# Row variance of an 8192 x 8192 matrix: whole 32 KiB rows per load, a quarter of each row on ScalarE, the last tile in pieces

## The chip, the cores and the metric

The kernel runs on one core of a Trainium2 chip. The metric is the device time of one execution in microseconds (us); the numbers quoted are medians of several runs. The profile is one execution recorded by the hardware; its span is about 1.8 us shorter than the device time, because launch and end lie outside it.

Engines in the profile: DVE is VectorE, ACT is ScalarE, POOL is GpSimd, PE and PEld are TensorE's matmul and weight load, SP is SyncE. A "q" behind the name is the engine's instruction queue, here issuing DMA transfers. All transfers of the core run on 16 DMA engines. A packet is the piece that one DMA engine moves at a time, here one stretch of one row; a chunk is the 512 columns that one `bn_stats` reads.

## The reference

```
def setup_inputs():
    return {"x": np.random.randn(8192, 8192).astype(np.float32)}

def reference(x):
    return np.var(x, axis=1)
```

So 268.4 MB are read once and 32 KB are written.

## The kernel before

128 rows, one per partition, make a tile; there are 64 tiles of 4 MiB. Each tile is loaded in two halves (16 KiB per row), one from SyncE's queue and one from ScalarE's. VectorE does all the arithmetic: 16 `bn_stats` of 512 columns (count, mean and sum of squared deviations of the even and of the odd elements) and one `bn_aggr`, which merges them to mean and variance. GpSimd copies the variance into a column of `var_all`. At the end TensorE transposes `var_all` so that the store writes 64 rows of 512 bytes.

```
    data = ctx.enter_context(tc.tile_pool(name="data", bufs=4))
    ...
    def issue_dma(t):
        xt = data.tile([P, nsub, FMAX], mybir.dt.float32)
        for c in range(CH):                                   # CH = 2
            lo = c * spc
            hi = lo + spc
            dma_eng[c % 2].dma_start(out=xt[:, lo:hi, :], in_=x_t[t, :, lo:hi, :])
    ...
    def compute(t):
        ...
        for j in range(nsub):                                 # nsub = 16
            nc.vector.bn_stats(out=st[:, j, :], in_=xt[:, j, :])
        nc.vector.bn_aggr(out=mv, in_=st)
        nc.gpsimd.tensor_copy(out=var_all[:, t : t + 1], in_=mv[:, 1:2])
    ...
    nc.tensor.transpose(vp, var_all, ident)
    nc.scalar.copy(vs, vp)
    nc.sync.dma_start(out=out_t, in_=vs)
```

## Time and profile before

| | before |
|---|---|
| device time, median (range) | 655.37 us (655.24 to 655.69) |
| span of the profile | 653.6 us |
| VectorE busy | 636.2 us, 97% |
| a tile on VectorE, start to start | 9.93 us |
| a tile on most of the 16 DMA engines | 9.79 us |

Lines of the page of the kernel before: its busy times, bytes moved per second in 40 slices of the span, its DMA queues, and the two costly groups (busy us, mean ns of one, idle time before them and what ended it).

```profile
span 653.6 us, 1512 instructions
PE 0.4 (0%) x1; PEld 0.1 (0%) x1; DVE 636.2 (97%) x1088; ACT 1.5 (0%) x2; POOL 12.4 (2%) x70
...
GB/s 369 433 430 425 427 432 428 425 431 428 427 428 430 427 427 430 427 427 428 428 426 431 427 429 427 426 429 428 428 427 430 427 428 429 429 425 430 429 222 2
...
q14 instruction: 12, 0.10, 0.0%
...
L61 DVE BATCH_NORM_STATS2 st<-xt 128x6 f32<-128x512 f32 x1024 | 610.1, 673 | 13.6 <-DMA xt<-in_x_dram 13.6
L63 DVE BATCH_NORM_AGGREGATE mv<-st 128x2 f32<-128x96 f32 x64 | 36.4, 570 | 0.1
```

VectorE waits for data only 13.6 us in all, nearly all of it for the first tile. So VectorE sets the pace. But the loads run at about 428 GB/s all the time until about 629 us, so there is little to gain below VectorE. (The mean of one `bn_stats`, 673 ns, is longer than its share of the pace, because two of them overlap; from start to start it is 0.59 us.)

The end of the kernel before, from its timeline (start us, duration us, engine, line, operation; in brackets the idle time before it):

```profile
630.32 9.53 DVE L61 BATCH_NORM_STATS2 st<-xt 128x6 f32<-128x512 f32 x16
...
640.26 8.93 DVE L61 BATCH_NORM_STATS2 st<-xt 128x6 f32<-128x512 f32 x15
...
649.29 0.59 DVE L63 BATCH_NORM_AGGREGATE mv<-st 128x2 f32<-128x96 f32 x1
649.94 0.18 POOL L64 COPY var_all<-mv 128x1 f32<-128x1 f32 x1 [9.36 <-DVE mv L63]
...
650.93 0.55 SPq L77 DMA_DIRECT2D out_dram<-vs  x1
```

The last two lines of the same kernel's issue list: kilobytes each, and median us from issue to landing.

```profile
xt<-in_x_dram SPq DMA_DIRECT2D x64, 2048.0 KB, 28.9
out_dram<-vs SPq DMA_DIRECT2D x1, 32.0 KB, 1.8
```

The store of 64 rows of 512 bytes takes 1.8 us from issue to landing. Between issue and the end of the span lie 2.65 us.

One view needs the raw records. A load is split over the 16 DMA engines, and each adds one to the load's semaphore (a counter that the waiting engine watches) when its part has landed. The trace holds the time of each of the 16, so one sees whether one engine lags:

| landing of (us) | first of 16 | 15th | 16th |
|---|---|---|---|
| tile 0, second half | 12.71 | 12.96 | 13.00 |
| tile 63, second half | 629.36 | 630.67 | 638.46 |

Fifteen engines are done at about 630 us and one 8 us later. The records say why: at nine times, about 70 to 80 us apart, an 8 KiB packet of kind "instruction" runs on queue 14, and the 16 KiB data packet next to it takes 1273 ns where others take 611 to 615. The last of the 16 completions steps back by about 0.96 us each time; over the whole run the mean is (9.10 - 0.29) / 9 = 0.98 us per fetch. VectorE has 1150 instructions with its waits, about nine blocks of 128. (The page counts 12 packets on queue 14. Beside the other three a data packet takes 961 to 1024 ns, and the last completion does not step back.)

### The profile page before, as it was taken

The page shows a single profiled execution, that of the slowest core. Times are in us where ns is not written, and L with a number is a line of the kernel's source. Part 1 is how long each engine was busy: PE and PEld are TensorE (multiplying, and loading weights), DVE is VectorE, ACT ScalarE, POOL GpSimd, SP SyncE. Part 2 cuts the span into 40 slices and gives each one's busy share as a digit, 9 for nine tenths or more (in the row PEclk, how much of TensorE's full clock was granted, in tenths as well). Part 3 has the DMA queues.
Part 4 walks back from the last instruction along what each step waited for, and adds up shares of the span by engine and source line. Part 5 has one row for each costly group of instructions (what it writes and reads, how often), then busy time and mean ns, then how long its engine had stood idle before and what let it go on. Part 6 is the DMA issues. An engine that isn't in the chain of part 4 may idle for free.

```text
span 653.6 us, 1512 instructions
## 1 busy us (share of the span) xinstructions
PE 0.4 (0%) x1; PEld 0.1 (0%) x1; DVE 636.2 (97%) x1088; ACT 1.5 (0%) x2; POOL 12.4 (2%) x70
## 2 busy tenths in 40 slices
PE   0000000000000000000000000000000000000000
PEld 0000000000000000000000000000000000000000
DVE  2999999999999999999999999999999999999997
ACT  0000000000000000000000000000000000000000
POOL 0000000000000000000000000000000000000000
DMA  8999999999999999999999999999999999999950
GB/s 369 433 430 425 427 432 428 425 431 428 427 428 430 427 427 430 427 427 428 428 426 431 427 429 427 426 429 428 428 427 430 427 428 429 429 425 430 429 222 2
DMA packets 18524, 268.57 MB, mean 411 GB/s; under 512 B 2064, under 2 KB 2128, under 8 KB 2128
## 3 DMA queue, kind: packets, MB, share of 16 engines
q1 hardware_dynamic: 9296, 134.25, 48.4%
q10 hardware_dynamic: 9216, 134.22, 48.2%
q14 instruction: 12, 0.10, 0.0%
HBM read 268.44 MB, written 0.03 MB: 411 GB/s over the span
## 4 chain that ended last, share of the span: by engine, by line
DVE 88%; DMA 6%; issue 5%; SPq 0%; PE 0%; ACT 0%; POOLq 0%; POOL 0%
DVE st L61 82%; DMA xt<-in_x_dram 6%; DVE mv L63 5%; SPq L54 0%; PE vp L74 0%; ACT vs L76 0%; POOLq L103 0%; POOL var_all L64 0%
## 5 line engine op out<-in xcount | busy, mean ns | idle before, releaser
L61 DVE BATCH_NORM_STATS2 st<-xt 128x6 f32<-128x512 f32 x1024 | 610.1, 673 | 13.6 <-DMA xt<-in_x_dram 13.6
L63 DVE BATCH_NORM_AGGREGATE mv<-st 128x2 f32<-128x96 f32 x64 | 36.4, 570 | 0.1
L64 POOL COPY var_all<-mv 128x1 f32<-128x1 f32 x64 | 11.7, 183 | 637.1 <-DVE mv L63 637.1
L76 ACT ACT_TABLE_LOAD x1 | 1.3, 1283 | 609.9 <-DMA xt<-in_x_dram 609.9
L74 PE MATMUL vp<-ident,var_all 128*64 128x128 f32 x1 | 0.4, 421 | 650.2 <-POOL var_all L64 650.2
L76 ACT COPY vs<-vp 64x128 f32<-64x128 f32 x1 | 0.3, 258 | 39.5 <-PE vp L74 39.5
masks.py:199 POOL TENSOR_SCALAR_AFFINE_SELECT ident<-ident 128x128 f32<-128x128 f32 x1 | 0.3, 292 | 0.1
L74 PEld LDWEIGHTS vp<-ident,var_all 128*64 128x64 f32 x1 | 0.1, 128 | 650.2 <-POOL var_all L64 650.2
masks.py:197 POOL MEMSET ident<- 128x128 f32 x1 | 0.2, 204 | 0.3 <-POOLq L92 0.3
L92 POOL MEMSET const-float32-0.0<- 128x1 f32 x1 | 0.1, 98 | 0.2 <-issue 0.2
L92 POOL MEMSET const-bfloat16-1.0<- 128x1 bf16 x1 | 0.1, 101 | 0.0
L92 POOL MEMSET const-uint8-127<- 128x1 uint8 x1 | 0.1, 101 | 0.0
L92 POOL MEMSET const-float32-1.0<- 128x1 f32 x1 | 0.1, 98 | 0.0
## 6 DMA issues: line engine op xcount, KB each, us to landing
xt<-in_x_dram ACTq DMA_DIRECT2D x64, 2048.0 KB, 29.1
xt<-in_x_dram SPq DMA_DIRECT2D x64, 2048.0 KB, 28.9
out_dram<-vs SPq DMA_DIRECT2D x1, 32.0 KB, 1.8
```

Of the source, the lines that this page charges most:

```text
L61: nc.vector.bn_stats(out=st[:, j, :], in_=xt[:, j, :])
L63: nc.vector.bn_aggr(out=mv, in_=st)
L64: nc.gpsimd.tensor_copy(out=var_all[:, t : t + 1], in_=mv[:, 1:2])
L74: nc.tensor.transpose(vp, var_all, ident)
L76: nc.scalar.copy(vs, vp)
L92: nc = _bacc.Bacc("TRN2", target_bir_lowering=False, num_devices=1)
```

## The change

The intent: take a quarter of the arithmetic off VectorE, make packets larger, and let little work remain behind the last byte.

```diff
-    CH = 2
-            dma_eng[c % 2].dma_start(out=xt[:, lo:hi, :], in_=x_t[t, :, lo:hi, :])
+    data = ... bufs=6
+        nc.sync.dma_start(out=xt, in_=x_t[t])               # 32 KiB rows, SyncE only
...
-        for j in range(nsub):
-            nc.vector.bn_stats(out=st[:, j, :], in_=xt[:, j, :])
+        for c in range(DC):                                 # DC = 12
+            bn(st, c, xt[:, o + c * F : o + (c + 1) * F])
+        k = st[:, 1:2]                                      # a mean from the first chunk
+        src = xt[:, o + DC * F : o + m]                     # the last 2048 columns
+        nc.scalar.activation(out=junk, in_=src, func=ACTF.Identity, bias=k, scale=-1.0,
+                             accum_out=s12[:, 0:1])         # sum of (k - x)
+        nc.scalar.activation(out=junk, in_=src, func=ACTF.Square, bias=k, scale=-1.0,
+                             accum_out=s12[:, 1:2])         # sum of (k - x)^2
+        ...   five GpSimd operations on 128x1: count, mean and squared deviations as one more entry of st
...
+    pieces = [4096, 2048, 1024, 512, 256, 256]              # the last tile
+    for w in pieces:
+        nc.sync.dma_start(out=xt[:, lo : lo + w], in_=x_t[t, :, lo : lo + w])
+    ...   63 tiles' variances: transpose and store as before
+    while lo < m:                                           # all 17 chunks on VectorE
+        w = F if m - lo > 512 else 256
+        bn(stl, i, xt[:, lo : lo + w])
+    nc.vector.bn_aggr(out=mv, in_=stl[:, 0 : i * 6])
+    nc.vector.tensor_copy(out=var_last[:, 0:1], in_=mv[:, 1:2])
+        nc.sync.dma_start(out=out_last[t], in_=var_last)    # 128 pieces of 4 bytes
```

More of the change, by code (lines that the diff above doesn't have):

```diff
@@ L7 @@
 from concourse._compat import with_exitstack
+FP32 = mybir.dt.float32
+ACTF = mybir.ActivationFunctionType
+ALU = mybir.AluOpType
 @with_exitstack
@@ L19 @@
     n, m = x.shape
-    FMAX = nc.vector.BN_STATS_FMAX
-    assert m % FMAX == 0
-    nsub = m // FMAX
-    assert n % P == 0
-    ntiles = n // P
-    x_t = x.rearrange("(t p) (s f) -> t p s f", p=P, f=FMAX)
-    out_t = out.rearrange("(t p) -> t p", p=P)
-    data = ctx.enter_context(tc.tile_pool(name="data", bufs=4))
-    stats = ctx.enter_context(tc.tile_pool(name="stats", bufs=8))
+    F = nc.vector.BN_STATS_FMAX
+    J = 1
+    NT = n // (P * J)
+    C = m // F
+    AC = 4
+    DC = C - AC
@@ L33 @@
+    NA = AC * F
+    T3 = 3
+    x_t = x.rearrange("(t p j) f -> t p (j f)", p=P, j=J)
+    out_tj = out.rearrange("(t q) -> t q", q=P * J)
+    out_last = out.rearrange("(t p j) -> t p j", p=P, j=J)
+    data = ctx.enter_context(tc.tile_pool(name="data", bufs=6))
+    stats = ctx.enter_context(tc.tile_pool(name="stats", bufs=6))
+    small = ctx.enter_context(tc.tile_pool(name="small", bufs=6))
     singles = ctx.enter_context(tc.tile_pool(name="singles", bufs=1))
     psum = ctx.enter_context(tc.tile_pool(name="psum", bufs=1, space=bass.MemoryType.PSUM))
-    outp = ctx.enter_context(tc.tile_pool(name="outp", bufs=1))
@@ L37 @@
-    var_all = singles.tile([P, ntiles], mybir.dt.float32)
-    ident = singles.tile([P, P], mybir.dt.float32)
-    make_identity(nc, ident)
-    dma_eng = [nc.sync, nc.scalar]
-    CH = 2
-    spc = nsub // CH
-    xts = [None] * ntiles
-    LOOK = 3
-    def issue_dma(t):
-        xt = data.tile([P, nsub, FMAX], mybir.dt.float32)
-        for c in range(CH):
-            lo = c * spc
-            hi = lo + spc
-            dma_eng[c % 2].dma_start(out=xt[:, lo:hi, :], in_=x_t[t, :, lo:hi, :])
-        xts[t] = xt
@@ L57, in compute @@
-    def compute(t):
-        xt = xts[t]
-        st = stats.tile([P, nsub, nc.vector.BN_STATS_DIM], mybir.dt.float32)
-        for j in range(nsub):
-            nc.vector.bn_stats(out=st[:, j, :], in_=xt[:, j, :])
-        mv = stats.tile([P, nc.vector.BN_AGGR_DIM], mybir.dt.float32)
-        nc.vector.bn_aggr(out=mv, in_=st)
-        nc.gpsimd.tensor_copy(out=var_all[:, t : t + 1], in_=mv[:, 1:2])
-    for t in range(ntiles):
-        issue_dma(t)
-        if t >= LOOK:
-            compute(t - LOOK)
@@ L70, with bn @@
-    for t in range(ntiles - LOOK, ntiles):
-        compute(t)
-    vp = psum.tile([ntiles, P], mybir.dt.float32)
-    nc.tensor.transpose(vp, var_all, ident)
-    vs = outp.tile([ntiles, P], mybir.dt.float32)
-    nc.scalar.copy(vs, vp)
-    nc.sync.dma_start(out=out_t, in_=vs)
+    var_all = singles.tile([P, J, NT], FP32)
+    var_last = singles.tile([P, J], FP32)
+    junk = psum.tile([P, NA], FP32)
+    def bn(st, at, src):
+        nc.vector.bn_stats(out=st[:, at * 6 : at * 6 + 6], in_=src)
@@ new lines, in row_stats @@
+    def row_stats(xt, j):
+        st = stats.tile([P, DC * 6 + T3], FP32)
+        s12 = small.tile([P, 2], FP32)
+        tmp = small.tile([P, 2], FP32)
+        o = j * m
+        for c in range(DC):
[6 more added lines that the diff above has]
+                             accum_out=s12[:, 1:2])
+        b = DC * 6
+        nc.gpsimd.memset(st[:, b : b + 1], float(NA))
+        nc.gpsimd.tensor_scalar(out=tmp[:, 0:1], in0=s12[:, 0:1], scalar1=1.0 / NA, scalar2=0.0,
+                                op0=ALU.mult, op1=ALU.add)
+        nc.gpsimd.tensor_tensor(out=st[:, b + 1 : b + 2], in0=k, in1=tmp[:, 0:1], op=ALU.subtract)
+        nc.gpsimd.tensor_tensor(out=tmp[:, 1:2], in0=s12[:, 0:1], in1=tmp[:, 0:1], op=ALU.mult)
+        nc.gpsimd.tensor_tensor(out=st[:, b + 2 : b + 3], in0=s12[:, 1:2], in1=tmp[:, 1:2], op=ALU.subtract)
+        return st
@@ new lines, in finish @@
+    def finish(st, t, j):
+        mv = small.tile([P, 2], FP32)
+        nc.vector.bn_aggr(out=mv, in_=st)
+        nc.gpsimd.tensor_copy(out=var_all[:, j, t : t + 1], in_=mv[:, 1:2])
+    pending = []
+    for t in range(NT - 1):
+        xt = data.tile([P, J * m], FP32, name="xt")
+        nc.sync.dma_start(out=xt, in_=x_t[t])
+        for j in range(J):
+            st = row_stats(xt, j)
+            pending.append((st, t, j))
+            if len(pending) > 1:
+                finish(*pending.pop(0))
@@ new lines @@
+    t = NT - 1
+    xt = data.tile([P, m], FP32, name="xt")
+    pieces = [4096, 2048, 1024, 512, 256, 256]
+    lo = 0
+    for w in pieces:
+        nc.sync.dma_start(out=xt[:, lo : lo + w], in_=x_t[t, :, lo : lo + w])
+        lo += w
+    finish(*pending.pop(0))
+    ident = singles.tile([P, P], FP32)
+    make_identity(nc, ident)
+    vs = singles.tile([NT - 1, P, J], FP32)
+    for j in range(J):
+        vp = psum.tile([NT - 1, P], FP32, name="vp")
+        nc.tensor.transpose(vp, var_all[:, j, 0 : NT - 1], ident)
+        nc.scalar.copy(vs[:, :, j], vp)
@@ new lines @@
+    nc.sync.dma_start(out=out_tj[0 : NT - 1], in_=vs)
+    stl = stats.tile([P, (C + 1) * 6], FP32, name="stl")
+    lo, i = 0, 0
+    while lo < m:
+        w = F if m - lo > 512 else 256
+        bn(stl, i, xt[:, lo : lo + w])
+        lo += w
+        i += 1
+    mv = small.tile([P, 2], FP32)
+    nc.vector.bn_aggr(out=mv, in_=stl[:, 0 : i * 6])
+    nc.vector.tensor_copy(out=var_last[:, 0:1], in_=mv[:, 1:2])
+    with nc.allow_non_contiguous_dma(reason="two values per partition"):
+        nc.sync.dma_start(out=out_last[t], in_=var_last)
```

## The prediction

> **What bounds it now.** Two limits are almost level. By the groups view VectorE (DVE) is busy 636.2 of 653.6 us: 16 bn_stats and one bn_aggr per 128-row tile, started every 9.93 us by the timeline; after its first tile it is never starved (13.6 us of DMA wait in all). The loads are hardly faster. In the DMA records each 16 KiB packet takes 611 to 615 ns, so a tile lands every 9.79 us on most of the 16 DMA engines. One engine loses about 0.96 us nine times (landings of a tile's 16 completions), each time just after an 8 KiB "instruction" packet on queue 14, about every 70 us; these fit VectorE's 1147 instructions in blocks of 128. That engine lands the last tile at 638.5, the others at about 630 (the stretch table shows DMA share 0.06, one engine of 16, after 630). VectorE starts that tile at 640.3 and the span ends at 653.6. So taking a quarter of the rows off VectorE does not buy 25%: the loads take over.
>
> **What changes.**
> - VectorE: 12 bn_stats and one bn_aggr, 12 x 0.59 + 0.49 = 7.6 us per tile, under the tile pitch. It will idle about 2 us per tile, waiting for DMA.
> - ScalarE: two passes over 2048 elements. The Trainium skill, "ScalarE: Activation LUTs", section on what ACT_TABLE_LOAD costs, gives about 1.99 us for one with a pointer bias (no run here shows it yet); about 4.3 us a tile with the accumulator reads, by estimate. GpSimd: five small ops near the measured 0.18 us. Both finish before VectorE's 12 chunks do, off the critical path.
> - DMA: 8 packets of 32 KiB per engine and tile rather than 16 of 16 KiB, and one completion write rather than two. The skill, "DMA: Bandwidth & Descriptors", "Where 436 GB/s comes from", gives 435.2 GB/s, that is 602 ns per 16 KiB; measured is 612. Taking the difference, 9 ns, as a cost per packet (the completion writes are also recorded at 9 ns), a 32 KiB packet takes about 1214 ns and a tile 9.72 us (estimate). That gives 62 x 0.07 = 4.5 us. One queue instead of two should cost nothing.
> - Instruction fetches: VectorE will have about 960 instructions, so 7 fetches, 6.7 us of lag on its engine.
> - Tail: the last tile is cut into shrinking pieces, but ScalarE does not help there. VectorE meets tile 62 whole at its landing, spends 7.1 + 0.5 us on it, then has all 17 chunks of the last tile: 15 x 0.59 + 2 x 0.33 = 9.5 us. So it ends about 7 us after the last piece landed, and the small pieces gain nothing.
>
> **Sum.** Tile 0 lands at 12.9; tile 62 at 12.9 + 62 x 9.72 + 6.7 = 622; VectorE done with chunks at 639.2; last aggregate, copy, store and closing 3.6 us (before: 649.2 to 653.6, less transpose and ScalarE copy): span about 643. Launch time outside the span 1.8 us as before: 644.6 us, a ratio of 0.984. Range 639 to 650. Chances: faster by over 2% 0.27, within 2% 0.69, slower 0.04.
>
> **Signs.** VectorE busy falls to about 500 us with some 120 us of DMA wait; 32 KiB packets near 1214 ns; tile pitch 9.72; about 7 instruction fetches followed by long packets on one engine; last piece landed about 632; VectorE running unbroken for about 17 us at the end; ScalarE busy about 270 us.
>
> **What would make it wrong.** A single queue leaving gaps between packets (pitch near 9.9: about 650); fetches that cost more or less behind 32 KiB packets, or extra lag on one engine from GpSimd's and ScalarE's added instructions; VectorE waiting for GpSimd in every aggregate.

## More of the kernel before

The experiments ran in three groups on three chips, with the kernel before beside each group.

The order of instructions on an engine need not be that of the program text: the tool that builds the kernel schedules them.

## The result

The changed kernel takes 649.84 us (649.6 to 650.48); the kernel before takes 655.37. The ratio is 0.9916, 95% interval 0.9902 to 0.993. (Ratios are the mean time of one kernel's fast runs over that of the other's fast runs of the same rounds, so not quite the ratio of the medians.)

Lines of the changed kernel's page that answer to those shown before:

```profile
span 647.9 us, 2020 instructions
PE 0.5 (0%) x1; PEld 0.2 (0%) x1; DVE 496.1 (77%) x838; ACT 265.5 (41%) x254; POOL 59.5 (9%) x384
...
GB/s 388 421 433 440 421 433 439 423 431 437 425 437 433 425 438 431 425 441 429 423 446 427 421 447 422 425 445 425 425 446 425 425 445 423 426 445 423 425 243 2
...
q14 instruction: 16, 0.13, 0.0%
...
L50 DVE BATCH_NORM_STATS2 st<-xt 128x6 f32<-128x512 f32 x756 | 454.8, 679 | 137.5 <-DMA xt<-in_x_dram 137.5
L63 ACT ACTIVATE junk<-xt,st 128x2048 f32<-128x2048 f32 x63 | 124.2, 1972 | 346.9 <-DVE st L50 346.9
```

VectorE lost 140 us of work and gained 124 us of waiting for data: it is no longer the limit in the loop. The loads are, and they are hardly faster than VectorE was.

The end of the changed kernel, from its timeline:

```profile
622.03 7.22 DVE L50 BATCH_NORM_STATS2 st<-xt 128x6 f32<-128x512 f32 x12 [1.90 <-DMA xt<-in_x_dram]
...
629.16 0.68 DVE L50 BATCH_NORM_STATS2 stl<-xt 128x6 f32<-128x512 f32 x1
...
630.15 9.00 DVE L50 BATCH_NORM_STATS2 stl<-xt 128x6 f32<-128x512 f32 x16
...
639.18 0.62 DVE L119 BATCH_NORM_AGGREGATE mv<-stl 128x2 f32<-128x102 f32 x1
639.83 0.15 DVE L120 COPY var_last<-mv 128x1 f32<-128x1 f32 x1
640.01 0.37 SPq L122 DMA_DIRECT2D out_dram<-var_last  x1
```

VectorE works with hardly a pause from 622.03 to 639.98. And its two stores in the issue list (for the first the profile gives no landing):

```profile
out_dram<-vs SPq DMA_DIRECT2D x1, 31.5 KB
out_dram<-var_last SPq DMA_DIRECT2D x1, 0.5 KB, 7.0
```

The last store moves 512 bytes and takes 7.0 us. The completions in the records:

| landing of (us) | first of 16 | 15th | 16th |
|---|---|---|---|
| tile 0 | 12.46 | 12.83 | 12.87 |
| tile 62 | 614.77 | 617.44 | 621.93 |
| last piece of tile 63 | 624.88 | 627.40 | 632.11 |
| last store | 642.94 | 646.58 | 646.97 |

So the 5.5 us gained come from three parts. In the loop, the landing of tile 62 at 621.93 us replaces VectorE's pace; at the end, VectorE has 29 chunks left from there, and 7.0 us of that work lies behind the last byte (632.11); and the store takes back 5 us.

### The profile page after: what moved, and what is told of

Same layout as the page of the kernel before. It is cut to its first block, busy times and chain, and to the rows that moved or that the text cites. A ratio compares the mean times of both kernels' runs of the same rounds, so it can differ in the third digit from the quotient of the medians.

```text
span 647.9 us, 2020 instructions
## 1 busy us (share of the span) xinstructions
PE 0.5 (0%) x1; PEld 0.2 (0%) x1; DVE 496.1 (77%) x838; ACT 265.5 (41%) x254; POOL 59.5 (9%) x384
## 4 chain that ended last, share of the span: by engine, by line
DVE 72%; another core or an unknown queue 17%; DMA 8%; issue 1%; DVEq 0%; SPq 0%
DVE st L50 66%; DMA xt<-in_x_dram 8%; DVE mv L78 4%; DVE stl L50 1%; SPq L84 0%; DVEq L78 0%; DVEq L50 0%; DVE mv L119 0%; DVE var_last L120 0%
## 5 line engine op out<-in xcount | busy, mean ns | idle before, releaser
L50 DVE BATCH_NORM_STATS2 st<-xt 128x6 f32<-128x512 f32 x756 | 454.8, 679 | 137.5 <-DMA xt<-in_x_dram 137.5
L63 ACT ACTIVATE junk<-xt,st 128x2048 f32<-128x2048 f32 x63 | 124.2, 1972 | 346.9 <-DVE st L50 346.9
L65 ACT ACTIVATE junk<-xt,st 128x2048 f32<-128x2048 f32 x63 | 124.2, 1972 | 2.0
L69 POOL TENSOR_SCALAR tmp<-s 128x1 f32<-128x1 f32 x63 | 12.1, 192 | 311.1 <-ACT junk L63 311.1
L78 DVE BATCH_NORM_AGGREGATE mv<-st 128x2 f32<-128x75 f32 x63 | 31.1, 494 | 6.4
L79 POOL COPY var_all<-mv 128x1 f32<-128x1 f32 x63 | 11.7, 185 | 153.8 <-DVE mv L78 153.8
L73 POOL TENSOR_TENSOR st<-s,tmp 128x1 f32<-128x1 f32 x63 | 12.1, 191 | 100.3 <-ACT junk L65 100.3
L71 POOL TENSOR_TENSOR st<-st,tmp 128x1 f32<-128x1 f32 x63 | 12.1, 191 | 5.2
L72 POOL TENSOR_TENSOR tmp<-s,tmp 128x1 f32<-128x1 f32 x63 | 12.0, 191 | 0.0
L63 ACT ACTIVATION_READ_ACCUMULATOR junk<-xt,st 128x1 f32 x63 | 11.8, 187 | 0.0
L65 ACT ACTIVATION_READ_ACCUMULATOR junk<-xt,st 128x1 f32 x63 | 11.7, 186 | 0.0
L50 DVE BATCH_NORM_STATS2 stl<-xt 128x6 f32<-128x512 f32 (+1 forms) x17 | 9.7, 645 | 0.0
L63 ACT ACT_TABLE_LOAD x1 | 1.3, 1283 | 12.9 <-DMA xt<-in_x_dram 12.9
L68 POOL MEMSET st<- 128x1 f32 x63 | 6.2, 99 | 0.3 <-POOLq L137 0.3
```

The source lines that it names most:

```text
L50: nc.vector.bn_stats(out=st[:, at * 6 : at * 6 + 6], in_=src)
L63: nc.scalar.activation(out=junk, in_=src, func=ACTF.Identity, bias=k, scale=-1.0, accum_out=s12[:, 0:1])
L65: nc.scalar.activation(out=junk, in_=src, func=ACTF.Square, bias=k, scale=-1.0, accum_out=s12[:, 1:2])
L68: nc.gpsimd.memset(st[:, b : b + 1], float(NA))
L69: nc.gpsimd.tensor_scalar(out=tmp[:, 0:1], in0=s12[:, 0:1], scalar1=1.0 / NA, scalar2=0.0, op0=ALU.mult, op1=ALU.add)
L71: nc.gpsimd.tensor_tensor(out=st[:, b + 1 : b + 2], in0=k, in1=tmp[:, 0:1], op=ALU.subtract)
```

## The experiments

The theory after the result: (1) VectorE limits the kernel before, and larger packets alone gain nothing; (2) in the changed kernel the loads limit the loop, at a rate set by a fixed cost per packet plus one DMA engine delayed by VectorE's instruction fetches; (3) the special last tile costs more than it saves, through VectorE's serial work and above all through the 4-byte store. Times below are medians; the kernel before ran beside each group, at 655.33 to 655.38.

### e1 and e8: the loads alone

e1 changes one line of the kernel before:

```diff
-    CH = 2
+    CH = 1
```

> The kernel before with only its loads changed: one 32 KiB row per partition on the SyncE queue. Theory (VectorE sets the pace, 9.93 us a tile): loads land faster, about 9.72 us a tile and the last tile near 634 instead of 638.5, but the time stays at 655, within 1 us. Rival (the loads set the pace): the time falls by some 4.5 us to about 651.

It took 667.05 us, ratio 1.0179. Neither expectation held. Two stretches of the timelines, first the kernel before and then e1, show a tile's aggregate and the next tile's chunks:

```profile
302.04 0.57 DVE L63 BATCH_NORM_AGGREGATE mv<-st 128x2 f32<-128x96 f32 x1
302.52 9.53 DVE L61 BATCH_NORM_STATS2 st<-xt 128x6 f32<-128x512 f32 x16
...
311.97 0.57 DVE L63 BATCH_NORM_AGGREGATE mv<-st 128x2 f32<-128x96 f32 x1
```

```profile
306.56 0.59 DVE L63 BATCH_NORM_AGGREGATE mv<-st 128x2 f32<-128x96 f32 x1
307.06 9.53 DVE L61 BATCH_NORM_STATS2 st<-xt 128x6 f32<-128x512 f32 x16
...
316.69 0.59 DVE L63 BATCH_NORM_AGGREGATE mv<-st 128x2 f32<-128x96 f32 x1
```

The same work repeats every 9.93 us before and every 10.13 us in e1. A tile in e1 costs 0.2 us more, 64 of them 12.8 us; the time rose by 11.7. With one load per tile instead of two the scheduler had put each aggregate right behind its own last chunk, whose result it reads; before, the first chunk of the next tile stood between them. So e1 changed two things. e8 repeats it with that order forced by a dependency:

```diff
     # e1, and:
+            inst = nc.vector.bn_stats(out=st[:, j, :], in_=xt[:, j, :])
+            if j == 0 and pending:
+                aggregate(*pending.pop(), inst)      # tile t-1, made to follow this chunk
```

> The one-piece loads again in the kernel before, now with VectorE's order forced to what it was: the aggregate of a tile behind the first chunk of the next one. In e1 the new loads had made the scheduler move the aggregate right behind its own last chunk, and VectorE's tile took 10.13 us instead of 9.93. Theory (VectorE sets the pace, and e1 lost its 11.7 us to that order): time 655 within 1 us, loads at 9.72 us a tile when not held back. Rival (32 KiB rows themselves slow VectorE): time stays near 667.

It took 655.00 us, ratio 0.9994 (0.9977 to 1.0011). The lines of its page read as in the kernel before:

```profile
span 653.3 us, 1387 instructions
PE 0.4 (0%) x1; PEld 0.1 (0%) x1; DVE 636.2 (97%) x1088; ACT 1.5 (0%) x2; POOL 12.6 (2%) x70
...
L61 DVE BATCH_NORM_STATS2 st<-xt 128x6 f32<-128x512 f32 x1024 | 610.1, 673 | 13.3 <-DMA xt<-in_x_dram 13.2
```

Its last tile landed at 633.54 us instead of 638.46, and nothing came of it. Part (1) stands. The order of one instruction per tile was worth 12 us.

### e2: packet size or number of queues

The changed kernel with each tile as two 16 KiB pieces per row, both from SyncE:

```diff
-        nc.sync.dma_start(out=xt, in_=x_t[t])
+        h = m // 2
+        nc.sync.dma_start(out=xt[:, 0:h], in_=x_t[t, :, 0:h])
+        nc.sync.dma_start(out=xt[:, h:m], in_=x_t[t, :, h:m])
```

> The changed kernel with each tile loaded in two pieces of 16 KiB rows, both on the SyncE queue. Theory (a fixed cost of about 9 ns a packet and completion write): packets of 611 to 615 ns, 9.79 us a tile as in the kernel before with its two queues, tile 62 some 4.5 us later, time about 654.3. Rival (packet size is immaterial, the number of queues matters): 9.72 us a tile and 649.8.

It took 653.20 us. Its packets took 611 to 615 ns and a half tile landed every 4.90 us, as with two queues in the kernel before; tile 62 was complete at 626.59, 4.66 us later than in the changed kernel. So packet size sets the rate and the number of queues does not. The time rose by 3.4 us rather than 4.5, but it is no clean measure of the loads, because here too the scheduler changed VectorE's order: each aggregate now stood before the next tile's first chunk and waited for GpSimd, 138.9 us in all. In the loop this did not hold the loads up (a half tile still landed every 4.90 us); before the last tile it is on the path:

```profile
621.89 7.19 DVE L50 BATCH_NORM_STATS2 st<-xt 128x6 f32<-128x512 f32 x12
...
631.28 0.49 DVE L78 BATCH_NORM_AGGREGATE mv<-st 128x2 f32<-128x75 f32 x1 [2.20 <-POOL st L73]
```

VectorE began tile 62 on its first half, at 621.89, lost 2.20 us to that wait, and was through with all chunks 2.1 us later than the changed kernel (aggregate at 641.32 against 639.18). The rest is a last store that landed 8.4 us after its issue instead of 7.0.

### e5 and e10: instruction fetches

e5 gives VectorE 806 tiny instructions more, placed in its idle time behind each tile's chunks:

```diff
+            if t < NT - 2:
+                nc.vector.tensor_copy(out=tiny, in_=st[:, DC * 6 - 1 : DC * 6])
+                for _ in range(12):
+                    nc.vector.memset(tiny, 0.0)
```

> The changed kernel with 13 tiny VectorE instructions more per tile (62 tiles, 806 instructions), which fit into VectorE's idle time of about 2 us per tile. Theory (each 128 VectorE instructions cost an 8 KiB instruction fetch that delays one DMA engine by about 0.96 us): some 6 fetches more, the last tile lands about 6 us later, time about 655.5. Rival (VectorE has slack, so its extra instructions are free): time stays at 649.8 within 1 us.

It took 656.03 us, 6.2 us more than the changed kernel. Lines of its page:

```profile
span 655.0 us, 2764 instructions
PE 0.5 (0%) x1; PEld 0.2 (0%) x1; DVE 540.5 (83%) x1644; ACT 265.5 (41%) x254; POOL 59.5 (9%) x384
...
q14 instruction: 21, 0.17, 0.1%
```

VectorE still waited 56.8 us for data, so it was not the limit. In the records the number of instruction packets followed by a data packet of 1.78 to 1.88 us (others take 1213 to 1218) rose from 7 to 13. The first of tile 62's 16 completions came at 614.89 (614.77 in the changed kernel), the last at 627.51 (621.93): 5.6 us for six fetches, on one DMA engine only. (The profiled run, at 656.81 us the slowest of the four, is 7.2 us over the changed kernel's profiled run; the other 1.5 us is the last store again, 8.5 us instead of 7.0.)

e10 is the control. The extra work goes to TensorE, on constant data:

```diff
+            if t < NT - 2:
+                for _ in range(7):
+                    nc.tensor.transpose(pt, idt[:, 0:1], idt)
```

> The control to e5: the same idea, but the extra instructions (434 transposes, a weight load and a matmul each, on constant data) go to TensorE, which has nothing else to do. Theory (each compute engine's instruction fetches fall on one DMA engine of its own): more fetches in all, but the DMA engine that VectorE's fetches delay stays the last, so time stays at 649.8 within 1 us. Rival (all instruction fetches fall on the same DMA engine): some 6 fetches more on it, time about 655.5 as in e5.

It took 649.69 us, as the changed kernel. So 868 more instructions on TensorE cost nothing, where 806 more on VectorE cost 6.2 us. The control is weaker than planned: TensorE fetched its instructions in three packets on another queue, not in six. After the first of them (19.5 us) the last of a tile's completions was 1.3 us behind the 15th, so the rival should have expected some 4 us. After the second (44 us) two completions lagged like that, so these fetches fell on different DMA engines, and the theory that each compute engine has one of its own does not hold for TensorE. The engine that VectorE's fetches delay stayed the last: for tile 62 it was 7.19 us behind the first, in the changed kernel 7.16.

The changed kernel's own trace holds a second control: besides VectorE's seven, eight instruction packets stand beside data packets of 1.57 to 1.63 us. By count they belong to GpSimd, ScalarE and SyncE (525, 380 and 143 instructions in blocks of 128; the trace does not name the engine). For tile 62 the 15th completion is only 2.7 us behind the first, and the last one's 6.75 us of lag are used up by VectorE's seven at 0.96 us each.

Lines of e10's page:

```profile
PE 84.5 (13%) x435; PEld 51.6 (8%) x435; DVE 496.0 (77%) x838; ACT 265.5 (41%) x254; POOL 59.6 (9%) x386
...
q14 instruction: 16, 0.13, 0.0%
q8 instruction: 3, 0.05, 0.0%
```

### e3, e4 and e6: the last tile

e3 stores the last 128 variances as one row:

```diff
-    nc.vector.tensor_copy(out=var_last[:, 0:1], in_=mv[:, 1:2])
...
-        nc.sync.dma_start(out=out_last[t], in_=var_last)
+    vpl = psum.tile([1, P], FP32, name="vpl")
+    nc.tensor.transpose(vpl, mv[:, 1:2], ident)
+    vsl = singles.tile([1, P], FP32)
+    nc.scalar.copy(vsl, vpl)
+    nc.sync.dma_start(out=out_tj[t : t + 1], in_=vsl)
```

> The changed kernel, but the last 128 variances are transposed on TensorE, copied by ScalarE and stored as one 512-byte row instead of 128 pieces of 4 bytes. Theory (the 4-byte store is what the prediction missed, 7.0 us from issue to landing against 1.85 us for the row store of the kernel before): the store lands in about 1.9 us, the transpose and copy cost about 0.9 us more than the removed VectorE copy, so the span falls by 4 to 4.5 us, to about 645.5 us in time. Rival (the store is slow because HBM writes at that moment are slow whatever their shape): the store still takes 6 to 7 us and the time rises by about 1 us.

It took 644.22 us, ratio to the kernel before 0.983: 5.6 us less than the changed kernel, from this alone. From its timeline:

```profile
639.38 0.62 DVE L119 BATCH_NORM_AGGREGATE mv<-stl 128x2 f32<-128x102 f32 x1
640.05 0.08 PEld L121 LDWEIGHTS vpl<-ident,mv 128*1 128x1 f32 x1 [9.13 <-DVE mv L119]
640.05 0.37 PE L121 MATMUL vpl<-ident,mv 128*1 128x128 f32 x1 [8.84 <-DVE mv L119]
640.46 0.26 ACT L123 COPY vsl<-vpl 1x128 f32<-1x128 f32 x1 [8.95 <-PE vpl L121]
640.74 0.25 SPq L124 DMA_DIRECT2D out_dram<-vsl  x1
```

The store is issued 0.7 us later than in the changed kernel, and the span, 642.7, ends 2.0 us after the issue. With the 4-byte pieces it was 7.9 us.

e4 drops the special last tile: all 64 tiles go through the loop, with one transpose and one row store.

```diff
-    for t in range(NT - 1):
+    for t in range(NT):
...
-    pieces = [4096, 2048, 1024, 512, 256, 256]   # and all that follows from it
```

> The changed kernel without any special last tile: all 64 tiles go through the loop, ScalarE has its quarter of the last one too, one transpose and one row store of 64x512 bytes. Theory: the last tile lands near 631.7, VectorE needs 7.2 us for 12 chunks, then aggregate, transpose, copy and store 3.7 us as in the kernel before; span about 643.5, time about 645.5, faster than the changed kernel by about 4.5 us. Rival (the shrinking pieces do hide work): the time is above 650.

It took 645.06 us, 4.8 us less than the changed kernel. So the special tail made the kernel slower than no tail at all. Without the 4-byte store (e3) it would have gained only 0.8 us over the plain loop. So of part (3) the store alone is shown to make it a loss.

e6 keeps the special tail but loads the last tile in two pieces:

```diff
-    pieces = [4096, 2048, 1024, 512, 256, 256]
+    pieces = [4096, 4096]
```

> The changed kernel with the last tile in two halves of 4096 columns instead of six shrinking pieces. Theory (VectorE has 17 chunks to do there and is the limit, so the small pieces gain nothing): VectorE works unbroken after tile 62, one chunk instruction fewer, time within 1 us of 649.8. Rival (shrinking pieces let the work end sooner): 2 us or more slower.

It took 649.92 us, no different from six pieces. (VectorE's 17 chunks stayed as they were, so "one chunk fewer" in the expectation was a slip.) It is VectorE's queue of work that ends late, not the data.

### e7 and e11: what makes the store slow

Both probes append stores to a scratch tensor, one after another, each shape twice (only the first overlaps the kernel's own last store, because nothing before it waits for that):

```diff
+            for dst, src in [ ... seven shapes ... ]:
+                nc.vector.memset(probe, 1.0)          # waits for the store before
+                nc.vector.tensor_copy(out=probe[:, 0:1], in_=var_last)
+                nc.sync.dma_start(out=dst, in_=src)
```

> The changed kernel with 14 stores to a scratch tensor after its own last store, each waiting for the one before, every shape twice: 128 pieces of 4 bytes side by side, at 64-byte, 512-byte and 4 KiB steps; 16 pieces of 4 bytes side by side; 128 rows of 512 bytes; one row of 512 bytes. Theory A (writes of less than 512 bytes to the same stretch of memory wait for each other): side by side takes about 7 us, at 512-byte and 4 KiB steps about 2 us. Theory B (the count of tiny pieces costs, wherever they go): all four 128-piece stores take about 7 us, the 16-piece one about 2 us. Both: the 512-byte rows about 1.9 us. The total time means nothing.

> A second probe of the slow store. e7 showed that 128 pieces of 4 bytes take 7.3 to 7.8 us side by side and 1.4 us at 64-byte steps. Here: 128 pieces at 4, 8, 16 and 32-byte steps, 64 and 32 pieces side by side, and 128 pieces of which only those of 4 neighbouring partitions lie side by side, the groups 4 KiB apart. Theory A (pieces that share 64 bytes wait for each other one by one): time falls with the number of pieces in 64 bytes, so about 7, 4, 2.5 and 2 us for the four steps, and 64 or 32 side by side stay near 7 us. Theory B (one after another within a longer stretch): time falls with the number of pieces side by side, 64 about 4 us, 32 about 2.7 us. The groups of 4: near 2 us in both. The total time means nothing.

From issue to the last completion, us, from the records (first and second time):

| store | us |
|---|---|
| 128 x 4 bytes side by side (e7; e11) | 7.5, 7.3; 7.1, 7.3 |
| 128 x 4 bytes, 8-byte steps (e11) | 2.8, 2.6 |
| 128 x 4 bytes, 16-byte and 32-byte steps (e11) | 1.4 in all four |
| 128 x 4 bytes, 64-byte, 512-byte and 4 KiB steps (e7) | 1.4 in all six |
| 64 x 4 bytes side by side (e11) | 6.3, 7.2 |
| 32 x 4 bytes side by side (e11) | 3.3, 2.9 |
| 16 x 4 bytes side by side (e7) | 1.3, 1.3 |
| 4 side by side, 32 such groups 4 KiB apart (e11) | 2.5, 2.8 |
| 128 x 512 bytes (e7) | 1.6, 1.6 |
| 1 x 512 bytes (e7) | 1.1, 1.1 |

Tiny pieces are not slow by number: 128 of them take 1.4 us when they lie 16 bytes or more apart. They are slow when many of them lie side by side: 16 take 1.3 us, 32 about 3, 64 or more 6.3 to 7.5. Neither theory of e11 fits: pieces that share 64 bytes at 16-byte steps pay nothing, against theory A, and 64 side by side take about as long as 128, against theory B. How the waiting comes about stays open. What it costs here is measured.

### e9: a version from the findings

ScalarE takes 6 of the 16 chunks of every tile, about the row's first element, so it need not wait for VectorE. It takes them in the last tile too. The last two tiles come in pieces, and one row store ends the kernel.

```diff
+    AC = 6
...
+        if t == NT - 2:
+            pieces = [4096, 4096]
+        if t == NT - 1:
+            pieces = [NA, 2048, 1536, 1024, 256, 256]      # NA = 6 * 512, ScalarE's part first
...
+        k = xt[:, 0:1]
+        src = xt[:, 0:NA]
...
+        nc.vector.bn_aggr(out=mv_all[:, t, :], in_=st[:, 0 : 3 + len(cuts) * 6])
...
+    nc.tensor.transpose(vp, mv_all[:, :, 1], ident)        # all 64 tiles, then one row store
```

> A version built from the findings: ScalarE takes 6 of 16 chunks of every tile, the last one included, about the row's first element (so it need not wait for VectorE); the last tile but one in two pieces and the last in six; one transposed row store for all 64 tiles; aggregates written where the transpose reads them. VectorE about 830 instructions, 6 fetches, tile 62 landed near 621; VectorE done with the chunks near 633; then 4.2 us to the end. Theory: span about 637.5, time about 639.5, ratio to the kernel before 0.976. If the tail does not shrink as computed: 643 or above.

It took 639.26 us (639.02 to 639.46), ratio to the kernel before 0.9754 (0.974 to 0.9769), as computed, and its result is correct. It changes several things at once, so it shows that the findings add up and not what each is worth. Lines of its page and of its timeline:

```profile
span 637.1 us, 1780 instructions
PE 0.4 (0%) x1; PEld 0.1 (0%) x1; DVE 414.2 (65%) x705; ACT 378.9 (59%) x258; POOL 51.9 (8%) x326
...
L78 DVE BATCH_NORM_STATS2 st<-xt 128x6 f32<-128x512 f32 x641 | 386.1, 678 | 197.7 <-DMA xt<-in_x_dram 197.7
```

```profile
626.87 6.09 DVE L78 BATCH_NORM_STATS2 st<-xt 128x6 f32<-128x512 f32 x11 [0.81 <-DMA xt<-in_x_dram]
...
633.07 0.47 DVE L80 BATCH_NORM_AGGREGATE mv_all<-st 128x2 f32<-128x69 f32 x1
...
634.34 0.55 SPq L86 DMA_DIRECT2D out_dram<-vs  x1
```

The last piece landed at 630.59 and VectorE's last chunk ended at 632.96: 2.4 us of arithmetic behind the last byte, against 7.0 in the changed kernel.

## Why the prediction was right, and where it was off

It said 644.6 us, 639 to 650, and most likely within 2%. The measured 649.84 lies in the range, at its edge, and the change is within 2%. That the range held was partly luck: the one cause for which it names about 650 is a single queue that leaves gaps, and that did not come; what used up the room was a store that it had not foreseen to be slow.

- *VectorE limits the kernel before, and the loads would take over.* Right. e8 shows that faster loads alone change nothing (655.00), and in the changed kernel VectorE waits 137.5 us, 12.9 of them for the first tile: 125 where about 120 were predicted.
- *A tile every 9.72 us from 32 KiB packets of 1214 ns, one queue as good as two.* Right: 1213 to 1218 ns and 9.71 us; e2 tells packet size from queue count. The ceiling came from the Trainium skill, "DMA: Bandwidth & Descriptors", "Where 436 GB/s comes from" (435.2 GB/s, by estimate 602 ns per 16 KiB); the trace is consistent with it plus 8 to 13 ns a packet, where the prediction took 9 (for a lower limit that the section also names, see the last section). The short packets of the changed kernel's last tile agree: 1, 2, 4 and 8 KiB took 46, 84, 159 and 313 ns (medians), 8 to 12 ns over their share of that rate. That one queue is enough is also what the section "Issuing engines are not separate DMA queues" of that page says.
- *Seven instruction fetches, 6.7 us of lag on one DMA engine.* Right: seven, and (621.93 - 614.77) - 0.41 = 6.75 us for tile 62. e5 adds six and the last completion of tile 62 comes 5.6 us later. The extra lag from GpSimd's and ScalarE's instructions that the prediction feared on that engine did not come.
- *ScalarE and GpSimd off the critical path.* Right. One pass took 1.97 us, where "ScalarE: Activation LUTs", "What ACT_TABLE_LOAD costs", gives about 1.99.
- *Tile 62 at 622, VectorE done with the chunks at 639.2, the small pieces gain nothing.* Right: 621.93 and 639.15; e6 shows the last.
- *"Last aggregate, copy, store and closing 3.6 us".* Wrong, and it is the whole miss. This stretch took 647.9 - 639.15 = 8.75 us. The store was assumed to land like the row store of the kernel before (1.85 us); with 128 pieces of 4 bytes side by side it took 7.0. e3 takes it away, at the price of 0.7 us for transpose and copy, and comes to 644.22, 0.4 us from the prediction. The prediction had costed that store from another store's duration, of another shape.

## What to carry to other kernels

Ask of a "last tile" special case what it does to the last engine and the last store, not only to the last load: here it idled ScalarE, left 7.0 us of work behind the last byte, and turned a 2 us store into a 7 us one. Cost a transfer by its shape, and test it alone where the trace has none like it; per-partition scalars are better transposed and stored as one row. When 16 DMA engines share a load, look at the last of them, and where the loads are the limit keep VectorE's instruction count low even where it has time to spare (e5). And a change to the loads alone can reorder the instructions, as in e1 and e2: look at the order before reading the time.

## What the Trainium skill lacked or had wrong

- "Runtime: NRT & Kernel Launch", "Instruction fetch mechanics", calls the cost of a fetch mostly hidden and speaks of 16 KiB blocks of 256 instructions. Here VectorE's fetches were 8 KiB packets about every 128 instructions (9 for 1150 instructions, 13 for 1708), and each delayed the same DMA engine, by 0.92 us (mean of 13 in e5) to 0.98 us (mean of 9 in the kernel before), which is not hidden where the loads are the limit: 6.75 us in the changed kernel, and 806 idle-time instructions cost 6.2 us in e5. TensorE's three packets together made 0.05 MB, which agrees with 16 KiB. The section does not say on which DMA engine a fetch falls: VectorE's all fell on one, TensorE's on different ones (e10).
- "DMA: Bandwidth & Descriptors" gives costs per packet only beside small packets and none for large ones. 16 KiB packets took 611 to 615 ns and 32 KiB packets 1213 to 1218 ns, so a tile took 9.79 or 9.71 us.
- The section "Where 436 GB/s comes from" of that page also says that for transfers between HBM and SBUF the HBM side, about 358 GB/s, is the limit. The one core here loaded at about 428 GB/s, so here the higher ceiling holds; no run shows two cores loading at once.
- "DMA: Bandwidth & Descriptors" says under "Specifications" that transfers under 512 bytes are read, modified and written. That does not tell the cost: 128 pieces of 4 bytes took 6.8 to 8.5 us side by side and 1.4 us at steps of 16 bytes or more. No page that was read has this.
- No page that was read gives the cost of `bn_stats` and `bn_aggr`: 0.59 us from start to start for 128x512 fp32, and 0.2 us more per tile where the aggregate stands right behind the last chunk it reads (10.13 against 9.93 us, e1 and e8).
